# Two chunks of the first mixer's output through the staging tiles, and the spreading of queries and keys in code order on VectorE

## The chip, the cores and the metric

The kernel runs on one core of a Trainium2 chip. The metric is the device time of one execution in microseconds (us), from runs on the chip; a separate profiled execution gives the trace that is read here. TensorE does the matrix products, VectorE and ScalarE the elementwise work, GpSimd (POOL) and SyncE (SP) mainly issue transfers (DMAs). Each engine works through its own list of instructions in order and waits where an input, or the place for a result, is not ready.

## The reference

One step of a two-layer encoder, for 1024 new frames of one stream and 16 frames of each of 8 running streams (1152 tokens of width 1024). Cut to what matters here:

```python
# layer 0
h = rmsnorm(x, norm_mix[0])
q, k, v, a, g = split(h @ w_in_ab)              # 8 heads of 64; u = a * sigmoid(g)
z = (q @ k.T) / 8
w = exp(log_sigmoid(z) + sum of log_sigmoid(-z) over the later keys)   # masked: stick-breaking
a_out = w @ v
c_out = silu(layernorm(depthwise_conv31(u)))
x = x + concat(a_out, c_out) @ w_out_ab
x = x + square(relu(rmsnorm(x) @ w_up)) @ w_down
# layer 1: the same with chunk-band attention as the mixer; then a final rmsnorm
```

All products are in float32; most are made as three products of a high and a low part (`SPLIT`), which a `split` writes: the high part by ScalarE, the low part by VectorE.

## The kernel before

The first mixer (`mixer0`) goes over four pairs of heads, `p` = 0 to 3. A run of the loop over `p` attends pair `p` and, as filling work for TensorE, projects the queries, keys and values of pair `p + 1`. VectorE also has the taps of the depthwise convolution (L735), up to the end of pair 2; the convolution's layer norm runs in pair 3.

A pair is attended in 8 jobs (2 heads, 4 blocks of 256 queries). For each 128 queries TensorE makes the scores `z` (L924 to L927), ScalarE takes two sigmoids (L928, L929), VectorE makes a running product over the keys (the scan of `kp`, L907) and multiplies (`sg`, L909). Then TensorE transposes the weights (`tpa`, L388), ScalarE copies them out (L390), TensorE multiplies by the values (`ava`, L398), and ScalarE and VectorE add the two halves (`ata` L406, `cpa` L410). The result goes to the DRAM tile `cat_d` (L363), for pair 3 straight into the tiles `cat`. The transposes and products of a pair's last block (`carry`) are named at the head of the next run.

`expand` spreads the queries and keys of a pair before it is attended. For each of the two heads it makes the keys' high part on ScalarE (L348) and their low part on VectorE (L351), each copied to the other 64 partitions by a POOL DMA (L349, L352), and the queries' high part (L350, ScalarE) and low part (L353, VectorE). It reads the projected tiles `sq` and `sk`.

In pair 3's run the filling work is the output projection over the first three chunks of the mixer's output (`part_out`, products `psoa` with weights `wo0a`). Its operand comes back from `cat_d`: `ready_chunks` loads a chunk of 128x1152 into one tile of the tag `sk` (of which there is one, the same that held the projected keys) and splits it in three parts of 384 columns into `cat`. The `cat` tiles take the places of the normed input `h`, which the projections read. Chunks 0 and 1 come first, then the first products of the output projection, then chunk 2 (`late`, behind the last block of pair 2), and the rest.

Weights go through `staging`: a tile of the tag `st` (three of them, 128x512) that SP loads, and then a split into a pair `hl` (four of them).

What sets the order: `merge` and `level` write out one order from lists of steps with planned costs. The framework then makes each engine's list from this order by a planning model: the earlier-named instruction has priority, but one whose inputs are planned to be there sooner goes ahead of it. `tc.keep_in_program_order(ins)` puts an instruction behind the one named last before it on its engine.

Of the kernel before, what the change touches and what calls it, by code (L numbers as in the profile page):

```python
# [11 lines left out]
ALU = mybir.AluOpType  # L12
# [7 lines left out]
TP = 1024  # L20
TAPS = (26, 36, 38, 24)
G = 384
NG = 3
# [17 lines left out]
def f(ap):  # L41
    return ap.bitcast(F32)
# [82 lines left out]
def tile_trunk(ctx, tc, ins, outs):  # L125
    nc = tc.nc
    ACT = nc.scalar.activation
    tt = nc.vector.tensor_tensor
    stt = nc.vector.scalar_tensor_tensor
# [4 lines left out]
    def pool(name):  # L134
        return tc.tile_pool(name=name, bufs=1, reuse_waits="tile")
# [40 lines left out]
    cat_d = [dram.tile([KC, P, T], F32, name=f"cat_d{l}") for l in range(2)]  # L176
# [6 lines left out]
    def split(hi, lo, src):  # L183

        ACT(hi, src, AF.Copy)  # L185
        return tt(lo, src, f(hi), ALU.subtract)  # L186
# [3 lines left out]
    def staging(src, name, n=512):  # L190
        st = sp.tile([P, 512], F32, tag="st", name=f"st_{name}")
        dma(st[:, :n], src)
        return st
# [54 lines left out]
    chunks = {}  # L248
# [90 lines left out]
        return steps  # L339


    def expand(qs, kd, kl, q, k):


        for i in range(2):
            own = slice(64 * i, 64 * i + 64)
            oth = slice(64 - 64 * i, 128 - 64 * i)
            ACT(kd[i][own], k[own, :TP], AF.Copy)  # L348
            nc.gpsimd.dma_start(kd[i][oth], kd[i][own])  # L349
            ACT(qs[i][own], q[own, :TP], AF.Copy, scale=0.125)  # L350
            tt(kl[i][own], k[own, :TP], f(kd[i][own]), ALU.subtract)  # L351
            nc.gpsimd.dma_start(kl[i][oth], kl[i][own])  # L352
            stt(qs[i][oth], q[own, :TP], 0.125, f(qs[i][own]), ALU.mult, ALU.subtract)  # L353

    class Cat:

# [298 lines left out]
    def mixer0():  # L655
        with ExitStack() as st:
# [8 lines left out]
            pp = Bufs(st.enter_context(pool("pair0")))  # L665
# [77 lines left out]
            def ag(c):  # L743
                return (chunk_steps(at[16 + c], got, ahead, h, ks, lambda ps, g: gate(c, ps, g), f"g{c}")
                        + chunk_steps(at[12 + c], got, ahead, h, ks, lambda ps, g: value(c, ps, g), f"a{c}"))
# [124 lines left out]
            def proj(p):  # L870
                steps = []
                for n, tag in enumerate(("sq", "sk", "sv")):
                    def evac(ps, g, n=n, tag=tag):
                        if g == 0:
                            S[tag, p] = pp.tile([P, T], F32, tag, f"{tag}0{p}")
                        if g < 2:
                            tt(S[tag, p][:, g * G:g * G + G], ps[:, :G], rstd[g], ALU.mult)
                        else:
                            ACT(S[tag, p][:, g * G:], ps[:, :G], AF.Copy)
                        if g == 2 and n:  # L880
                            put(outs["sb_k" if n == 1 else "sb_v"][p], S[tag, p])
                    steps += chunk_steps(at[4 * n + p], got, ahead, h, ks, evac, f"p{p}{n}")
                return steps

            def expand_qk(p):
                q, k = S["sq", p], S["sk", p]
                expand(qs, kd, kl, q, k)
                S["qn"] = pp.tile([P, P], F32, "qn", f"qn0{p}")
                S["kn"] = pp.tile([P, P], F32, "kn", f"kn0{p}")
                ACT(S["qn"], q[:, TP:], AF.Copy, scale=0.125)  # L890
                ACT(S["kn"], k[:, TP:], AF.Copy)
# [69 lines left out]
            qs, kd, kl = ([ep.tile([P, TP], F32R, f"{n}{i}", f"{n}{i}") for i in range(2)] for n in "qkl")  # L961
# [3 lines left out]
            carry, cat_t = [], None  # L965
            for p in range(4):
                S["p"] = p
                expand_qk(p)
                if p < 3:
                    fill = proj(p + 1)  # L970
                    if p < 2:
                        fill[10:10] = ag(p + 2)
                    n = TAPS[p + 1]
                    mix, now, taps = [], taps[:n], taps[n:]
                else:
                    cat_t = new_hs("cat0")
                    (first, fill), now = part_out(0, range(3), pp, cat_t), []
                    for s in taps:
                        s.pe = 900.0
                    mix = taps + conv_norm(lambda: (conv_pool.close(), Bufs(st.enter_context(pool("ln")), t1=3, yl=5))[1],  # L980
                                           cat_t)
                cat = Cat(0, p, wk, cat_t)
                jobs = attend(p, cat)
                body, left = pipeline(jobs[1:], jobs[0][2])
                steps = carry + [jobs[0][0]] + [Step(327.0, lambda p=p, g=g: expand_v(p, g)) for g in range(NG)]
                if p == 3:
                    late, = ready_chunks(0, [2], pp, cat_t)
                    late.name, late.after, late.lag = "ready", carry[-1].name, 3000.0
                    fill[0].after, fill[0].lag = "ready", 5000.0
                    fill = ready_chunks(0, range(2), pp, cat_t) + first + [late] + fill  # L990
                steps += [jobs[0][1]] + body
                carry = left
                if p == 3:
                    steps += carry
                cs = sample_out(cat, wk, p)
                load = sample_caches(0, p, cp)
                sample = two_samples(*(sample_steps(0, p, bg, S, wk, load, soft, cs) for bg in range(2)))
                run(level(merge(steps, sample, fill, mix), now))
            return cat_t

    def conv_norm(new_pool, cat_t):

        steps = []

        pools = []

        def norm(g):
            box = {}

            def load():  # L1010
                if g == 0:
                    pools.append(new_pool())
                box["y"] = [pools[0].tile([P, G], F32, "yl", f"yl{g}{c}") for c in range(4)]
                for c in range(4):
                    put(box["y"][c], cat_d[0][4 + c, :, g * G:g * G + G])

            def centre():
                yl = box["y"]
                mu = bank(f"mu{g}")
                for c in range(4):  # L1020
                    mm(mu[:, :G], ones, yl[c], start=c == 0, stop=c == 3)
                for c in range(4):
                    stt(yl[c], mu[:, :G], -1.0 / 512, yl[c], ALU.mult, ALU.add)

            def squares():
                yl, box["acc"] = box["y"], None
                for c in range(4):
                    box["acc"] = add_square(box["acc"], yl[c], pools[0], f"l{g}{c}")

            def scale():  # L1030
                box["r"] = pools[0].tile([P, G], F32, "r", f"rl{g}")
                diag, box["rows"], _ = rstd_of(box["r"], pools[0], box["acc"], 1.0 / 512, LN_EPS, f"l{g}")
                diag(box["acc"])

            def out(c):
                y = box["y"][c]
                tt(y, y, box["r"], ALU.mult)
                s = pools[0].tile([P, G], F32, "t1", f"ls{g}{c}")
                gg, bb = cvec[:, 1, c:c + 1], cvec[:, 2, c:c + 1]
                ACT(s, y, AF.Sigmoid, bias=bb, scale=gg)  # L1040
                ACT(y, y, AF.Identity, bias=bb, scale=gg)
                tt(y, y, s, ALU.mult)
                split(cat_t[g][1][0][:, c, :], cat_t[g][1][1][:, c, :], y)

            name = f"ln{g}"
            return ([Step(50.0, load, 0.0, f"l{name}"),
                     Step(2600.0, centre, 1900.0, f"c{name}", f"l{name}", 4000), Step(500.0, squares, 1400.0),
                     Step(700.0, scale, 1200.0, f"s{name}", f"c{name}", 5000),
                     Step(800.0, lambda: box["rows"](), 0.0, None, f"s{name}", 2500)]
                    + [Step(300.0, lambda c=c: out(c), 1500.0) for c in range(4)])  # L1050

        for g in range(NG):
            steps += norm(g)
        return steps

    def ready_chunks(layer, chunks, pp, cat_t):

        steps = []
        for c in chunks:
            def go(c=c):  # L1060
                cr = pp.tile([P, T], F32, "sk", f"cr{layer}{c}")
                dma(cr, cat_d[layer][c])
                for g in range(NG):
                    hi, lo = (x[:, c % 4, :] for x in cat_t[g][c // 4])
                    split(hi, lo, cr[:, g * G:g * G + G])
            steps.append(Step(300.0, go))
        return steps
# [878 lines left out]
```

## Time and profile before

| | |
|---|---|
| time before, median of 3 runs | 2752.49 us (2751.73 to 2756.9) |
| the profiled execution | 2748.28 us |
| its span, first to last instruction | 2746.5 us |
| TensorE busy | 2666.7 us (97%) |
| VectorE busy | 2090.2 us (76%) |
| ScalarE busy | 1388.1 us (51%) |

The first mixer takes the first 550 us or so of the span. In the rows below PE is TensorE, PEld its weight loads, DVE VectorE, ACT ScalarE; L351 is line 351 of the kernel. Times are counted from the start of the span. "[4.14 <-DVE sg L909]" says that the engine was idle for 4.14 us before the instruction, and what ended that.

### The profile page before, as it was taken

Reading aid. Unit: us, or ns where it says so; the run is one execution under the profiler, and the core shown is the slowest. Engines: PE = TensorE matmul, PEld = TensorE weight load, DVE = VectorE, ACT = ScalarE, POOL = GpSimd, SP = SyncE. Lnnn points to the kernel's source line nnn. Section 1 sums busy time; section 2 is a strip of 40 time slices with the busy share of each in tenths; the row PEclk is TensorE's granted clock in tenths of the full one; section 3 lists DMA queues with packets and bytes.
Section 4 is the critical chain, followed back from the end, with each engine's and each line's share of the span. In section 5 each row is a group of like instructions: output and inputs, shape, how many; then the busy total and the mean of one; then the engine's idle time right before and its main releaser. Section 6 shows DMA issues by size and latency. Waiting matters only on the chain.

```text
span 2746.5 us, 50585 instructions
## 1 busy us (share of the span) xinstructions
PE 2666.7 (97%) x19362; PEld 2553.7 (93%) x19362; DVE 2090.2 (76%) x4117; ACT 1388.1 (51%) x2906; POOL 328.2 (12%) x599
## 2 busy tenths in 40 slices
PE   8999898999999999999999999998999999999998
PEld 8987776799999999999999999997999999999998
DVE  8999998888777755768577777778787777647577
ACT  5344457755444543435355555556555545434344
POOL 1000101041111100000011111110221111100001
PEclk9999999999999999999999999999999999999999
DMA  4434446454344377435444444446534334674344
GB/s 158 124 113 141 122 137 228 144 176 140 142 143 145 133 271 248 118 102 174 141 138 144 133 139 139 132 134 231 180 127 144 143 140 144 232 259 134 96 125 145
DMA packets 173203, 422.90 MB, mean 154 GB/s; under 512 B 25968, under 2 KB 53808, under 8 KB 170912
## 3 DMA queue, kind: packets, MB, share of 16 engines
q1 hardware_dynamic: 135696, 288.38, 33.4%
q0 software_dynamic: 37120, 131.27, 13.9%
q8 instruction: 152, 2.49, 0.4%
q14 instruction: 91, 0.75, 0.1%
q10 hardware_dynamic: 144, 0.02, 0.0%
HBM read 289.60 MB, written 117.34 MB: 148 GB/s over the span
## 4 chain that ended last, share of the span: by engine, by line
PE 71%; DVE 4%; ACT 2%; DMA 1%; issue 1%; DVEq 0%; SPq 0%; ACTq 0%; POOLq 0%
PE pd L1690 26%; PE um L1461 25%; PE psc L225 10%; PE avc L467 2%; PE tpc L455 2%; PE zc L1201 1%; PE zc L1202 1%; PE psoa L225 1%; PE so L602 1%; PE zs L568 1%; DVE xr L1367 0%; PE psob L225 0%; DMA cr<-cat_d 0%; ACT s L1168 0%; ACT whc L185 0%
## 5 line engine op out<-in xcount | busy, mean ns | idle before, releaser
L225 PE MATMUL psc<-h,hl_wc 128*128 128x384 f32 x1728 | 327.2, 340 | 0.0
L225 PEld LDWEIGHTS psc<-h,hl_wc 128*128 128x128 f32 x1728 | 296.9, 188 | 13.3 <-issue 10.9
L1461 PE MATMUL um<-sl,hl_m 128*128 128x288 f32 x1548 | 240.8, 296 | 0.0
L1461 PEld LDWEIGHTS um<-sl,hl_m 128*128 128x128 f32 x1548 | 218.2, 189 | 0.0
L1690 PE MATMUL pd<-tm,hl_wd 128*128 128x288 f32 x1584 | 214.7, 295 | 0.0
L1690 PEld LDWEIGHTS pd<-tm,hl_wd 128*128 128x128 f32 x1584 | 211.3, 189 | 0.0
L735 DVE SCALAR_TENSOR_TENSOR y<-u,dw,y 128x1024 f32<-128x1024 f32 (+1 forms) x232 | 178.1, 810 | 0.6
L225 PE MATMUL psp<-h,hl_wi 128*128 128x384 f32 x864 | 165.7, 344 | 0.0
L1468 ACT ACTIVATE hdm<-hdm 128x288 f32<-128x288 f32 x192 | 84.7, 442 | 156.5 <-DVE hdm L1467 154.8
L225 PEld LDWEIGHTS psp<-h,hl_wi 128*128 128x128 f32 x864 | 150.8, 191 | 6.8 <-issue 6.0
L186 DVE TENSOR_TENSOR tm<-xr,tm 128x576 fp32r<-128x576 f32 (+1 forms) x120 | 86.1, 718 | 92.4 <-ACT tm L185 92.3
L185 ACT ACTIVATE tm<-xr 128x576 fp32r<-128x576 f32 (+1 forms) x120 | 77.6, 647 | 94.7 <-PE pd L1690 76.2
L1168 ACT ACTIVATE s<-s,mxc 128x640 f32<-128x640 f32 (+4 forms) x128 | 88.8, 694 | 60.2 <-DVE mxc L1165 58.5
L1461 PE MATMUL um<-sl,hl 128*128 128x288 f32 x756 | 119.1, 296 | 0.0
L1690 PE MATMUL pd<-th,hl_wd 128*128 128x288 f32 x792 | 113.9, 297 | 4.0 <-DVE th L186 3.9
L1690 PEld LDWEIGHTS pd<-th,hl_wd 128*128 128x128 f32 x792 | 108.4, 190 | 4.9 <-DVE th L186 4.3
L1690 PE MATMUL pd<-xr,hl_wd 128*128 128x288 f32 x792 | 112.3, 296 | 0.0
L1690 PEld LDWEIGHTS pd<-xr,hl_wd 128*128 128x128 f32 x792 | 107.8, 190 | 0.0
L1461 PEld LDWEIGHTS um<-sl,hl 128*128 128x128 f32 x756 | 106.4, 188 | 0.8
L1690 PE MATMUL pd<-tm,hl 128*128 128x288 f32 x768 | 104.9, 295 | 0.0
L1690 PEld LDWEIGHTS pd<-tm,hl 128*128 128x128 f32 x768 | 103.1, 188 | 0.0
L185 ACT ACTIVATE whc<-tpc 128x512 fp32r<-128x512 f32 (+1 forms) x144 | 72.3, 522 | 46.6 <-PE tpc L455 44.8
(526 smaller groups left out, 6632.1 us busy)
## 6 DMA issues: line engine op xcount, KB each, us to landing
xr<-hb_d SPq DMA_DIRECT2D x208, 288.0 KB, 3.0
xr<-in_w_up_dram SPq DMA_DIRECT2D x64, 512.0 KB, 4.3
hb_d<-hdm POOLq DMA_DIRECT2D x96, 288.0 KB, 2.4
hb_d<-t POOLq DMA_DIRECT2D x96, 288.0 KB, 2.4
wm<-in_w_down_dram SPq DMA_DIRECT2D x64, 256.0 KB, 4.0
st_wd<-in_w_down_dram SPq DMA_DIRECT2D x64, 256.0 KB, 3.7
st_wc<-in_w_in_c_dram SPq DMA_DIRECT2D x44, 256.0 KB, 3.0
xm_d<-xo POOLq DMA_DIRECT2D x16, 576.0 KB, 3.5
```

The lines of the kernel that those rows point to most:

```text
L185: ACT(hi, src, AF.Copy)
L186: return tt(lo, src, f(hi), ALU.subtract)
L225: mm(ps()[:, :G], hl[:, a, at:at + P], act[g][k // 4][b][:, k % 4, :], start=n == 0, stop=n == len(todo) - 1)
L455: nc.tensor.transpose(tp[:, c0 + q * P:c0 + (q + 1) * P], blocks.get(j, tile_q), ident)
L467: mm(st["av"][:, o0:o0 + n], vs[:, j, i].rearrange("p a d -> p (a d)"), src[:, c0:c0 + n], start=st["done"] == 0, stop=st["done"] == nmm - 1)
L568: mm(box["z"][at // 512][own, at % 512:at % 512 + kw], qb[:, own], k[:, b * kw:b * kw + kw], start=True, stop=True)
L602: mm(box["o"][own, 0:P], wt[k4][:, c:c + 32], v[:, at:at + P], start=False, stop=k4 == nz - 1 and j == 3)
L735: stt(src if j == CW - 1 else dst, src, wj, dst, ALU.mult, ALU.add)
L1168: ACT(s[:, :n], s[:, :n], AF.Exp, bias=mx, scale=-1.0, accum_out=tot)
L1461: mm(banks[b, n][:, :TQ], w[:, a, c * P:c * P + P], combo(key, c)[:, h, n * TQ:n * TQ + TQ], start=k < 3 and c == 0 and i == 0, stop=c == ...
L1468: ACT(y, y, AF.Relu)
L1690: mm(ps, w[:, a, m * P:m * P + P], b[:, h, (n - ns[0]) * TQ:(n - ns[0]) * TQ + TQ], start=first and s == 0, stop=j == NJ - 1 and s == 2, s ...
```

## The change

It does two things. `expand` gets an argument `pin`; in the first mixer, for pairs 1 to 3, it is `keep_in_program_order`, and it is laid on the two VectorE instructions of each head (keys' and queries' low parts). And chunks 0 and 1 of the first mixer's output come back in pieces of 384 columns by a new function, `ready_pieces`: each piece is loaded into a staging tile and split from there; a step is one piece and not one chunk. Chunk 2 stays as it was.

```diff
-    def expand(qs, kd, kl, q, k):
+    def expand(qs, kd, kl, q, k, pin=lambda ins: ins):
...
-            tt(kl[i][own], k[own, :TP], f(kd[i][own]), ALU.subtract)
+            pin(tt(kl[i][own], k[own, :TP], f(kd[i][own]), ALU.subtract))
             nc.gpsimd.dma_start(kl[i][oth], kl[i][own])
-            stt(qs[i][oth], q[own, :TP], 0.125, f(qs[i][own]), ALU.mult, ALU.subtract)
+            pin(stt(qs[i][oth], q[own, :TP], 0.125, f(qs[i][own]), ALU.mult, ALU.subtract))
...
-                expand(qs, kd, kl, q, k)
+                expand(qs, kd, kl, q, k, *([tc.keep_in_program_order] if p else []))
...
-                    fill = ready_chunks(0, range(2), pp, cat_t) + first + [late] + fill
+                    fill = ready_pieces(0, range(2), cat_t) + first + [late] + fill
...
+    def ready_pieces(layer, chunks, cat_t):
+
+        def go(c, g):
+            st = staging(cat_d[layer][c, :, g * G:g * G + G], f"cr{layer}{c}{g}", G)
+            split(*(x[:, c % 4, :] for x in cat_t[g][c // 4]), st[:, :G])
+
+        return [Step(100.0, lambda c=c, g=g: go(c, g)) for c in chunks for g in range(NG)]
```

## Rows read from the trace of the kernel before

**Rows 1.** Busy us (x instructions) of PE, PEld, DVE, ACT, POOL by stretch; clock; DMA.
```profile
214.00:335.00 121.00, 109.22 (x800) 93.60 (x800) 116.44 (x157) 55.51 (x129) 11.64 (x21) 0.97 0.45 130
335.00:420.00 85.00, 81.00 (x640) 67.56 (x641) 83.66 (x110) 47.07 (x113) 7.53 (x14) 0.98 0.41 126
...
446.00:580.00 134.00, 127.16 (x868) 108.98 (x865) 116.35 (x209) 100.95 (x215) 20.44 (x28) 0.99 0.56 187
```
**Rows 2.** Waits of TensorE, 90 to 450 us: total us, times, longest.
```profile
PE tpa L388 <- DVE sg L909: 21.5, 9, 6.2
```
**Rows 3.** VectorE in order of time at pair 0 to 1: start, us, instruction.
```profile
211.51 1.21 DVE L351 TENSOR_TENSOR l<-sk,k 64x1024 fp32r<-64x1024 f32 x1
...
214.95 1.22 DVE L351 TENSOR_TENSOR l<-sk,k 64x1024 fp32r<-64x1024 f32 x1
216.20 1.22 DVE L909 TENSOR_TENSOR sg<-sg,kp 128x1023 f32<-128x1023 f32 x1
```
**Rows 4.** ScalarE in order of time at pair 2 to 3.
```profile
421.07 0.62 ACT L929 ACTIVATE kp<-z 128x512 f32<-128x512 f32 x1
```
**Rows 5.** VectorE in order of time at pair 2 to 3.
```profile
422.08 1.22 DVE L351 TENSOR_TENSOR l<-sk,k 64x1024 fp32r<-64x1024 f32 x1
423.34 1.22 DVE L353 SCALAR_TENSOR_TENSOR q<-sq,q 64x1024 fp32r<-64x1024 f32 x1
424.59 2.29 DVE L907 TENSOR_TENSOR_SCAN kp<-kp,ones 128x1024 f32<-128x1024 f32 x1
...
426.91 1.23 DVE L909 TENSOR_TENSOR sg<-sg,kp 128x1023 f32<-128x1023 f32 x1
...
428.43 0.42 DVE L410 TENSOR_TENSOR cpa<-ava,ata 64x256 f32<-64x256 f32 x1
...
431.20 1.50 DVE L186 TENSOR_TENSOR cat<-cr,cat 128x384 fp32r<-128x384 f32 x3 [1.29 <-ACT cat L185]
```
**Rows 6.** TensorE in order of time at pair 2 to 3.
```profile
428.19 0.87 PE L388 MATMUL tpa<-ident,sg 128*128 128x128 f32 x6 [4.14 <-DVE sg L909]
431.22 0.69 PE L225 MATMUL psoa<-cat,hl_wo0a 128*128 128x384 f32 x1 [2.15 <-ACT cat L185]
...
439.48 2.44 PE L225 MATMUL psoa<-cat,hl_wo0a 128*128 128x384 f32 x12
...
444.30 0.33 PE L924 MATMUL z<-k,q 128*128 128x128 f32 x1
```
**Rows 7.** SP's DMA issues in order of time, 360 to 450 us.
```profile
365.02 0.89 SPq L192 DMA_DIRECT2D st_wo0a<-in_w_out_ab_dram  x2
...
423.33 0.34 SPq L1062 DMA_DIRECT2D cr<-cat_d  x1
...
432.72 0.33 SPq L1062 DMA_DIRECT2D cr<-cat_d  x1
```
**Rows 8.** DMA issues, 420 to 442 us: KB each, median us to landing.
```profile
cr<-cat_d SPq DMA_DIRECT2D x2, 576.0 KB, 6.7
...
st_wo0a<-in_w_out_ab_dram SPq DMA_DIRECT2D x2, 192.0 KB, 5.5
l<-l POOLq DMA_DIRECT2D x1, 256.0 KB, 7.0
```
**Rows 9.** Busy us by stretch, as rows 1, around pair 2 to 3.
```profile
422.00:440.00 18.00, 11.71 (x61) 7.01 (x61) 9.75 (x15) 6.74 (x15) 6.32 (x11) 0.81 1.08 348
...
428.00:444.30 16.30, 13.95 (x80) 8.73 (x80) 7.69 (x17) 7.71 (x16) 3.77 (x7) 0.79 0.83 284
```
**Rows 10.** Spreading that ran early on VectorE: first and last of five.
```profile
153.24 1.22 DVE L353 SCALAR_TENSOR_TENSOR q<-sq,q 64x1024 fp32r<-64x1024 f32 x1
...
396.21 1.21 DVE L351 TENSOR_TENSOR l<-sk,k 64x1024 fp32r<-64x1024 f32 x1
```
**Rows 11.** DMA issues, 360 to 400 us, as rows 8.
```profile
st_wo0a<-in_w_out_ab_dram SPq DMA_DIRECT2D x4, 192.0 KB, 2.5
...
l<-l POOLq DMA_DIRECT2D x1, 256.0 KB, 2.9
```

## The prediction, made before the result was known

> **What bounds the kernel now.** I read the busy times by stretch first, because the whole page only says that TensorE is busy 97% of the span. The stretch in question is the first mixer. While pairs 1 and 2 are attended (214 to 420 us), VectorE is busy in 116.44 of 121 and 83.66 of 85 us: it is idle for 4.56 + 1.34 = 5.9 us of 206, and TensorE for 11.78 + 4.00 = 15.8 us. After the mixer's hand-over to pair 3 (446 to 580 us) it is TensorE that is full, 127.16 of 134 us [rows 1]. So up to 420 us VectorE sets the pace, and time saved at the hand-over should be carried through what follows. The list of waits says what TensorE waits for between 90 and 450 us: 21.5 us in 9 waits for the last VectorE step of a block's stick-breaking weights (`sg`, L909) [rows 2].
>
> Then I read VectorE and TensorE in order of time around the two hand-overs that the change touches most.
>
> At pair 0 to 1, VectorE spreads the next pair's keys (L351, 1.21 us) ahead of the last block's scan, and a second time (1.22 us) between the scan and the product that TensorE's transposes need; the product starts at 216.20 [rows 3]. That is the 6.2 us wait, the longest of rows 2.
>
> At pair 2 to 3 it is plainer. The scan's input was finished by ScalarE at 421.07 + 0.62 = 421.69 [rows 4], but VectorE runs L351 at 422.08 and L353 at 423.34 first; the scan starts at 424.59, the product ends at 426.91 + 1.23 = 428.14 [rows 5], and TensorE's transposes resume at 428.19 after 4.14 us of idleness [rows 6]. Next TensorE waits 2.15 us for chunk 0 of `cat`, and its last 12 products with `cat` start only at 439.48; the first product of pair 3's scores is at 444.30, behind them in TensorE's order [rows 6]. Chunk 0 is late because its load was issued at 423.33, when L351 had read the keys' tile `sk` that it lands in, and chunk 1 is late because it shares that tile: issued at 432.72 [rows 7]. Both take 6.7 us to land, where transfers of a third the size take 5.5 us [rows 8]: from 422 to 440 us the 16 DMA engines are busy 1.08 of the time, so everything lands late [rows 9].
>
> **The pin.** It removes and adds no instruction; it moves twelve (four for each of pairs 1 to 3). By the order in which the code names the work, the last VectorE instruction named before `expand_qk(p)` is the addition at L410 of the previous pair's last block but one (428.43 at pair 2 to 3 [rows 5]), so the four now run in a row behind it: 4 x 1.22 = 4.9 us. Some had run far earlier: the first is at 153.24, the last of that kind at 396.21, five in all [rows 10].
>
> Count the work ahead of the product that ends at 428.14. Before, all twelve stand ahead of it. After, pair 3's four stand behind it, the eight of pairs 1 and 2 still ahead. So VectorE has 4 x 1.22 = 4.9 us less to do before that point. Of this, 424.59 - 422.08 = 2.5 us is the direct part (the scan follows the taps at once). The other 2.4 us (pair 3's first two, the later of them at 396.21 [rows 10]) counts only if TensorE and ScalarE follow, for ScalarE's 421.69 leaves no more than 0.4 us otherwise. They can: TensorE's waits of rows 2 are waits for VectorE. From below the value is 2.5 us, if the rest is lost in the order of things; from above, the 4.9 us plus what late work can fill of VectorE's idle time, taken as 2.4 of the 5.9 us of rows 1, so 7.3. I take 4.9, since VectorE is idle for only 1.34 of 85 us in the stretch just before [rows 1]. The gain at pair 0 to 1 (216.20 - 213.82 = 2.4 us, if a scan of 2.29 us [rows 5] starts at 211.51) is not an extra: the four moved instructions run right after it, in the same full stretch.
>
> What the pin makes late: the spread keys' second half is copied by a DMA behind L351, and pair 3's scores need it. L351 would run near 424, and with 7.0 us of landing [rows 8] and POOL's issue it is there by 432: ahead of 444.30, so it costs nothing unless the scores are wanted 12 us sooner than now. In POOL's queue the copy stands ahead of the loads of the convolution's rows, which are wanted after it. At a quieter hand-over the copy takes 2.9 us [rows 11], and there the next pair's projection fills TensorE meanwhile.
>
> **The staging.** Two loads of 576 KB into `sk` become six of 192 KB into the `st` tiles; the same six splits of 128x384 remain (1.50 us of VectorE for a chunk's three [rows 5], as many on ScalarE). SP issues four more loads, at some 0.35 us each [rows 7], 1.4 us on an engine that is mostly idle; it lies beside SP's waiting. What falls away is the wait for `sk`: the first three pieces can land as soon as staging tiles are free, and the output weights (`st_wo0a`), which come behind them in the code, took theirs at 365.02 already [rows 7], with 2.5 us to land in that quiet time [rows 11]. So chunk 0 is there when the projection lets go of the `h` tiles it is written to, and the 2.15 us wait goes.
>
> But the kernel has three staging tiles. The second three pieces and then the output weights must wait until the first pieces are split. The chain is: three lo splits 1.5, landing 2.5 to 5.5, splits 1.5, weights landing 2.5 to 5.5, their split some 1.1 (two such instructions); 9.1 us in quiet and 15.1 in crowded time [rows 5, 8, 11]. If the lo splits start near 419, when VectorE finishes its taps in the shifted kernel, the 18 products can start at 428 to 434, ahead of 439.48. If they come behind the four pinned instructions (near 429), at 438 to 444.
>
> For the hand-over after the product I read one stretch: from 428 to 444.30 TensorE is busy 13.95 of 16.30 us at a granted clock of 0.79, so it loses 2.35 us idle and up to 0.21 x 16.3 = 3.4 us because part ran at 1.2 and not 2.4 GHz, after it had been idle since 424 [rows 9]. At best the change gains both, 5.8 us; at worst the chain costs 6 us or more. I take 1.1 us, half the wait for chunk 0: in the middle of the first case, since the chain still makes TensorE wait for something.
>
> **A rule weighed.** In rows 8 and 11 a piece of 192 KB lands in 2.5 us in quiet time and 5.5 us in crowded time. The Trainium skill, "DMA: Bandwidth & Descriptors", section "Anatomy of one DMA", gives a fixed cost of about 2.0 us for each transfer plus its bytes over 436 GB/s, which speaks against cutting two transfers into six. By it a piece (197 kB) would take 2.45 us, which the quiet row bears out; if all six were waited for one by one, it would be four more fixed costs, 8 us more and a slower kernel. The sum here does without it: three pieces are in flight at once, and in crowded time the row decides.
>
> **Sum.** 4.9 + 1.1 = 6.0 us. The profiled execution took 2748.28 us (span 2746.5 and 1.8 around it); less 6.0 that is 2742.3. The median of the runs is 2752.49, 4.2 above the profiled one; in its terms the forecast is 2746.5.
>
> **Rivals.** A change under 0.2% (5.5 us) can hardly be told from none here.
> - *The staging chain replaces the wait (slower).* If VectorE takes the lo splits behind the pinned four and the loads land at crowded times, the output products start at 444 instead of 439.48. They end at 448, the scores follow 2.4 us later, near 450.4 and not 444.30, and an idle TensorE drops to 1.2 GHz again as in rows 9, for some 2.5 us: 6.1 + 2.5 = 8.6 us slower, 2761. It decides once the weights are split after 439.5. For it speak the three tiles; against it, that TensorE's order may put pair 3's scores first. Chance 0.15.
> - *The chain eats the gain.* The weights come near 437 to 440; 4 of the 6 us go. 2750.5. Chance 0.2.
> - *Only moved.* VectorE fills the freed places with taps that wanted to be run anyway, and the last scan comes no more than 2.5 us sooner, with the wait for chunk 1 in place of that for chunk 0: 2750. Rows 1 speak for it (work is conserved), rows 4 and 5 against. Chance 0.15.
>
> **Numbers.** The forecast has 0.5, with its own range from 4 to 11 us less, 2741.5 to 2748.5; about a fifth of it lies within 0.2%. Faster: 0.42. Same: what is left of the forecast, 0.08, and both middle rivals, 0.35, so 0.43. Slower: 0.15. The range takes in the forecast's lower half and two thirds of the slower case: 2741 to 2757.
>
> **What would show it.** Right: at pairs 0 to 1 and 2 to 3 the scan follows the last tap with no L351 or L353 ahead; the four stand in a row behind L410; the list of waits for `sg` falls from 21.5 to some 16 us; three pieces land before 400 us; the first scores of pair 3 come near 438. Wrong: `st_wo0a` loads issued after 430 with TensorE waiting for their splits, or lo splits of `cat` ahead of the last scan, which would give its gain back.

## The result, and the profile after

The changed kernel takes 2762.23 us in the median of 7 runs, the kernel before 2752.49 us beside it; the ratio is 1.0028, with a 95% interval of 1.0018 to 1.0038. So it is slower by 0.28%, 7.7 us by the ratio. (The ratio is taken over all the runs and is not the quotient of the two medians, which lie 9.7 us apart; all sizes below go by ratios.) The forecast was 2746.5 us, with a range up to 2757: wrong in sign and outside the range. The profiled execution took 2757.41 us, 9.1 more than the one before, and its span grew by the same 9.1, to 2755.6.

Where this arises is read from events that both traces have. Attention of pair 2 begins (its first `vt` transposes) 3.3 us earlier than before, the last `sg` of pair 2 ends 1.4 us earlier, and the first scores of pair 3 come 9.5 us later (453.78 against 444.30 [rows 6]). What follows keeps a delay of some 9 to 11 us to the end. The whole loss lies between the last `sg` and the first scores: 10.9 us in one hand-over.

The list of TensorE's waits between 90 and 460 us names it: total us, times, longest.

```profile
PE tpa L388 <- DVE sg L909: 16.7, 7, 5.1
PE psoa L225 <- ACT hl_wo0a L185: 12.5, 1, 12.5
```

The waits for `sg` fell from 21.5 to 16.7 us, as forecast for the pin. But there is a new wait of 12.5 us, for the high part of the output weights. Before, at this place, TensorE waited 2.15 us for `cat` [rows 6].

TensorE of the changed kernel in order of time (start, us, instruction, and in brackets how long it was idle and what ended that):

```profile
426.81 1.54 PE L388 MATMUL tpa<-ident,sg 128*128 128x128 f32 x6 [4.41 <-DVE sg L909]
...
440.85 2.29 PE L225 MATMUL psoa<-cat,hl_wo0a 128*128 128x384 f32 x6 [12.50 <-ACT hl_wo0a L185]
...
449.90 1.51 PE L225 MATMUL psoa<-cat,hl_wo0a 128*128 128x384 f32 x6
...
453.78 0.33 PE L924 MATMUL z<-k,q 128*128 128x128 f32 x1
```

The transposes resume 1.4 us earlier than in [rows 6]; then nothing until 440.85. The wait grew by 12.50 - 2.15 = 10.35 us, and the gap ahead of the transposes by 4.41 - 4.14 = 0.27: together 10.6 of the 10.9.

What the weights waited for stands in SP's issues (start, time over which they were issued, count):

```profile
332.79 0.34 SPq L192 DMA_DIRECT2D st_cr<-cat_d  x1
...
363.61 0.88 SPq L192 DMA_DIRECT2D st_cr<-cat_d  x2
...
422.38 1.91 SPq L192 DMA_DIRECT2D st_cr<-cat_d  x3
...
433.33 12.17 SPq L192 DMA_DIRECT2D st_wo0a<-in_w_out_ab_dram  x7
```

Chunk 0's three pieces took the three staging tiles at 332.79 and 363.61, when these came free, because the code names them ahead of the output weights. Their parts go where the projection's `h` lies until late in pair 2: ScalarE made the high parts at 414.45 and VectorE, behind its taps, the low parts at 421.81. So the three staging tiles were held for 58 to 89 us. At 422.38 the second chunk's pieces took them over, and the output weights, which before were loaded at 365.02 [rows 7], were issued at 433.33.

VectorE in order of time shows why the second round lasted until then:

```profile
420.35 1.54 DVE L735 SCALAR_TENSOR_TENSOR u<-u,dw,y 128x1024 f32<-128x1024 f32 x2
421.81 1.49 DVE L186 TENSOR_TENSOR cat<-st_cr,cat 128x384 fp32r<-128x384 f32 x3
423.21 2.28 DVE L907 TENSOR_TENSOR_SCAN kp<-kp,ones 128x1024 f32<-128x1024 f32 x1
425.53 1.23 DVE L909 TENSOR_TENSOR sg<-sg,kp 128x1023 f32<-128x1023 f32 x1
427.04 0.42 DVE L410 TENSOR_TENSOR cpa<-ava,ata 64x256 f32<-64x256 f32 x1
427.49 1.22 DVE L351 TENSOR_TENSOR l<-sk,k 64x1024 fp32r<-64x1024 f32 x1
428.74 1.22 DVE L353 SCALAR_TENSOR_TENSOR q<-sq,q 64x1024 fp32r<-64x1024 f32 x1
429.97 1.22 DVE L351 TENSOR_TENSOR l<-sk,k 64x1024 fp32r<-64x1024 f32 x1
431.23 1.22 DVE L353 SCALAR_TENSOR_TENSOR q<-sq,q 64x1024 fp32r<-64x1024 f32 x1
432.48 1.50 DVE L186 TENSOR_TENSOR cat<-st_cr,cat 128x384 fp32r<-128x384 f32 x3
440.83 1.54 DVE L186 TENSOR_TENSOR hl_wo0a<-st_wo0a,hl_wo0a 128x384 fp32r<-128x384 f32 x3 [6.85 <-ACT hl_wo0a L185]
```

Two things are to be seen. Chunk 0's low parts (421.81) run ahead of the last scan, which starts at 423.21 and not when the taps end. And the second chunk's low parts wait behind the four pinned instructions, until 432.48. ScalarE had made the first high part at 426.00, as soon as its piece landed, and the third at 430.05:

```profile
426.00 0.52 ACT L185 ACTIVATE cat<-st_cr 128x384 fp32r<-128x384 f32 x1 [3.53 <-DMA st_cr<-cat_d]
...
430.05 0.52 ACT L185 ACTIVATE cat<-st_cr 128x384 fp32r<-128x384 f32 x1 [0.74 <-DMA st_cr<-cat_d]
...
440.27 1.50 ACT L185 ACTIVATE hl_wo0a<-st_wo0a 128x384 fp32r<-128x384 f32 x3 [9.22 <-DMA st_wo0a<-in_w_out_ab_dram]
```

The weights, issued from 433.33 on, were split from 440.27: 6.9 us for the first of them. So the chain from chunk 0's low parts to the first product is 440.85 - 421.81 = 19.0 us.

Busy us (x instructions) of PE, PEld, DVE, ACT, POOL by stretch of the changed kernel, then the granted clock and the DMA share:

```profile
422.00:440.00 18.00, 1.95 (x9) 1.31 (x8) 11.78 (x15) 3.03 (x6) 6.79 (x12) 0.59 0.91 267
...
425.60:445.80 20.20, 6.49 (x28) 4.77 (x29) 10.27 (x14) 5.54 (x11) 4.32 (x8) 0.50 0.72 218
...
446.00:580.00 134.00, 127.06 (x877) 104.79 (x876) 113.25 (x207) 99.37 (x214) 16.80 (x25) 0.99 0.55 184
```

From 422 to 440 us TensorE is busy 1.95 us where it was 11.71 [rows 9]. The clock is 0.50, the lower level of 1.2 GHz, for 20.2 us, and TensorE is busy for 6.49 of them. From 446 to 580 us TensorE is as full as before, 127.06 against 127.16 of 134 [rows 1], so the delay is not made up there.

### The profile page after: what moved, and what is told of

Read it like the earlier page. It is cut to its first block, busy times and chain, and to the rows that moved or that the text cites. A ratio compares the mean times of both kernels' runs of the same rounds, so it can differ in the third digit from the quotient of the medians.

```text
span 2755.6 us, 50598 instructions
## 1 busy us (share of the span) xinstructions
PE 2669.1 (97%) x19362; PEld 2556.0 (93%) x19362; DVE 2090.3 (76%) x4117; ACT 1388.5 (50%) x2906; POOL 328.8 (12%) x599
## 4 chain that ended last, share of the span: by engine, by line
PE 78%; DVE 12%; ACT 4%; issue 3%; DMA 3%; POOL 0%; SPq 0%; DVEq 0%; ACTq 0%; POOLq 0%
PE pd L1698 26%; PE um L1469 25%; PE psc L225 10%; DVE y L735 3%; PE psp L225 3%; PE avc L467 2%; DVE kp L907 2%; PE tpc L455 2%; PE psoa L225 1%; PE f L225 1%; PE zc L1209 1%; PE psob L225 1%; PE zc L1210 1%; DVE sg L909 1%; PE so L602 1%
## 5 line engine op out<-in xcount | busy, mean ns | idle before, releaser
L225 PEld LDWEIGHTS psc<-h,hl_wc 128*128 128x128 f32 x1728 | 296.8, 188 | 13.3 <-issue 10.9
```

Source lines behind the costliest of these rows:

```text
L225: mm(ps()[:, :G], hl[:, a, at:at + P], act[g][k // 4][b][:, k % 4, :], start=n == 0, stop=n == len(todo) - 1)
```

## The experiments

Each kernel was timed in turns with the kernel before; the ratio is to that, with its 95% interval. The diffs are against the changed kernel, but for "The rows on SP in the kernel before". Between two experiments I compare ratios. Times within one trace are single executions, and those differ by some 2 us where nothing was edited: the first scan starts between 106.92 and 109.06 us in the twelve traces, and with the rows on SP in the kernel before, an edit that lies behind it, the last `sg` of pair 2 starts at 428.89, where [rows 5] have 426.91. Five of the ten measured times (the pieces alone, weights first without the pin, the rows on SP, chunk 0 alone, and the last one) lie 0.2 to 1.7 us outside the range expected; each still falls on the side of the theory that its waits bear out.

### The pin alone

```diff
-                    fill = ready_pieces(0, range(2), cat_t) + first + [late] + fill
+                    fill = ready_chunks(0, range(2), pp, cat_t) + first + [late] + fill
```

> The pin alone; both chunks come back through sk as before. Theory S (the serial chain through three staging tiles makes the change slower): the 12.5 us wait of TensorE for the split output weights is gone, since those weights find free staging tiles near 365 us again. Theory P (the pin itself makes it slower): the wait stays, and the time stays near 2762. Under S there is still a price: the load of chunk 0 waits until the second L351 has read sk, which the pin puts near 431 and not 423, so the first product with cat comes some 5 us later than before the change: 2752 to 2758. Lower than 2750 would say that the pin alone is a gain.

Measured: 2755.11 us beside 2752.93, ratio 1.0007 [0.9996, 1.0017]. The waits of TensorE, 90 to 460 us:

```profile
PE psoa L225 <- ACT cat L185: 8.8, 1, 8.8
...
PE tpa L388 <- DVE sg L909: 15.8, 7, 5.2
```

The wait for `sg` is down by 5.7 us, but the wait for chunk 0 is 8.8 where it was 2.15 [rows 6]. Its load was issued at 429.14, and at 423.33 before [rows 7]: it lands in the keys' tile `sk`, and the pinned L351 reads that tile from 427.83 to 429.05. So the pin moves the last reading of `sk` back by some 6 us and with it chunk 0. This cost of the pin by itself the prediction did not have. It also says what the staging is good for: it takes chunk 0 off `sk`.

### The pieces alone

```diff
-                expand(qs, kd, kl, q, k, *([tc.keep_in_program_order] if p else []))
+                expand(qs, kd, kl, q, k)
```

> The pieces alone, no pin. Under S the output weights still come last through the three tiles, so TensorE waits for them at pair 2 to 3; but chunk 1's low parts no longer stand behind four spreading instructions on VectorE (2 to 5 us of the chain), so the wait is 6 to 10 us and not 12.5, and the time 2754 to 2760. Under P: no wait for the weights and the time of before, 2752, or less.

Measured: 2760.21 us beside 2752.93, ratio 1.0026 [1.0017, 1.0035]. The waits, and SP's issues:

```profile
PE tpa L388 <- DVE sg L909: 22.6, 8, 6.2
PE psoa L225 <- ACT hl_wo0a L185: 9.4, 1, 9.4
```

```profile
433.15 1.64 SPq L192 DMA_DIRECT2D st_cr<-cat_d  x3
...
437.93 9.39 SPq L192 DMA_DIRECT2D st_wo0a<-in_w_out_ab_dram  x7
```

The staging makes the kernel slower by itself, as much as the whole change. Without the pin, chunk 0's low parts run behind the spreading and the last `sg`, at 432.56, so the second chunk's pieces are issued at 433.15 and the weights at 437.93; the wait is shorter only because TensorE arrives at it later. The chain sets the start of the products in both cases, so the pin is worth nothing that shows: 1.0026 without, 1.0028 with.

### The output weights claim the staging tiles first

`first` begins with the step that stages the output weights; it is named ahead of the pieces, and nothing else changes.

```diff
-                    fill = ready_pieces(0, range(2), cat_t) + first + [late] + fill
+                    fill = first[:1] + ready_pieces(0, range(2), cat_t) + first[1:] + [late] + fill
```

> As the change, but the step that loads the first two output weights is named ahead of the pieces, so they take staging tiles first. Under S the 12.5 us wait for their split goes and 8 to 12 us come back: 2750 to 2754, or less if the pin's gain (2.4 us at each hand-over) is kept. Under P it stays near 2762.

Measured: 2752.26 us beside 2752.93, ratio 0.9996 [0.9985, 1.0007]. Against the change this is 0.0032 of the time, 8.8 us, from the order of two steps: the whole loss. TensorE in order of time:

```profile
419.62 0.84 PE L225 MATMUL psoa<-cat,hl_wo0a 128*128 128x384 f32 x3
...
424.23 0.98 PE L388 MATMUL tpa<-ident,sg 128*128 128x128 f32 x6 [3.56 <-DVE sg L909]
...
437.90 1.08 PE L1021 MATMUL mu<-yl,ones 128*128 128x384 f32 x2 [2.38 <-DMA yl<-cat_d]
...
440.54 0.48 PE L924 MATMUL z<-k,q 128*128 128x128 f32 x1
```

The first products with `cat` run at 419.62, even ahead of the last `sg`, and the first scores come at 440.54, 3.8 us ahead of [rows 6]. Yet the time is that of the kernel before. In this execution (2754.80 us, 2.5 above the median) the windows say where the 3.8 us went:

```profile
434.00:438.00 4.00, 1.62 (x9) 0.68 (x7) 0.00 (x0) 0.00 (x0) 0.00 (x0) 1.00 1.07 320
...
440.40:444.00 3.60, 2.76 (x19) 1.62 (x16) 1.70 (x5) 3.04 (x8) 0.55 (x1) 0.50 0.57 164
444.00:448.00 4.00, 3.40 (x15) 3.10 (x14) 3.11 (x8) 3.54 (x11) 0.00 (x0) 0.50 0.66 191
448.00:452.00 4.00, 3.31 (x18) 2.45 (x19) 4.00 (x6) 3.51 (x9) 0.00 (x0) 0.50 0.88 341
```

TensorE waits 2.38 us for the convolution's rows `yl`, and its clock then is 0.50 in the next stretches, while it is busy for 9.47 of the 11.6 us from 440.40 to 452. In the kernel before the clock was 1.00 there:

```profile
438.00:456.00 18.00, 15.49 (x107) 11.07 (x106) 14.15 (x25) 12.76 (x32) 0.55 (x1) 1.00 0.67 210
```

That the clock costs as much in other executions of this kernel is not shown.

### Weights first, without the pin

```diff
-                expand(qs, kd, kl, q, k, *([tc.keep_in_program_order] if p else []))
+                expand(qs, kd, kl, q, k)
...
-                    fill = ready_pieces(0, range(2), cat_t) + first + [late] + fill
+                    fill = first[:1] + ready_pieces(0, range(2), cat_t) + first[1:] + [late] + fill
```

> Pieces with the weights named first, and no pin: against e3_weights_first it gives what the pin is worth when the staging chain is out of the way. Under S 2750 to 2755, and the pin's worth up to 5 us either way; under P faster than e3_weights_first by 8 us or more.

Measured: 2755.34 us beside 2752.93, ratio 1.0008 [0.9999, 1.0017]. Against weights first with the pin (0.9996) the pin is worth 0.0012, 3.3 us; the intervals overlap, so it is a likely size only. Against the pieces alone (1.0026) the order of the two steps is worth 0.0018, 5.0 us, without the pin too.

### Weights first, and the convolution's rows on SP's queue

The loads of `yl` stand in POOL's queue (`put`); here SP issues them (`dma`).

```diff
-                    fill = ready_pieces(0, range(2), cat_t) + first + [late] + fill
+                    fill = first[:1] + ready_pieces(0, range(2), cat_t) + first[1:] + [late] + fill
...
-                    put(box["y"][c], cat_d[0][4 + c, :, g * G:g * G + G])
+                    dma(box["y"][c], cat_d[0][4 + c, :, g * G:g * G + G])
```

> As e3_weights_first, and the loads of the convolution's rows (yl) are issued by SP and not by POOL, where they stood behind the pinned keys' copies and landed at 437.9. Theory Q (with the staging chain out of the way, these loads are the next thing TensorE waits for, because the pin delays POOL's queue): the 2.4 us wait of the mu products goes, pair 3's scores come before 440, and the time falls to 2747 to 2750. Rival C (the crowded DMA engines set it, whoever issues): the rows land as late, and the time stays within 2 us of e3_weights_first, 2750 to 2754.

Measured: 2745.32 us beside 2754.0, ratio 0.9969 [0.996, 0.9979]. This is faster than both kernels. In weights first, POOL issued the last two loads only at 429.70, behind the copy of the pinned keys, which waited for VectorE's L351:

```profile
429.18 0.53 POOL L352 DMA_DIRECT2D l<-l  x1 [1.06 <-DVE l L351]
429.70 1.09 POOL L1015 DMA_DIRECT2D yl<-cat_d  x2
```

With the loads on SP, four are issued between 423.23 and 428.44:

```profile
423.23 5.21 SPq L1015 DMA_DIRECT2D yl<-cat_d  x4
```

TensorE in order of time, and its clock by stretch:

```profile
432.36 2.20 PE L1021 MATMUL mu<-yl,ones 128*128 128x384 f32 x6 [0.39 <-DMA yl<-cat_d]
...
438.67 0.33 PE L924 MATMUL z<-k,q 128*128 128x128 f32 x1
```

```profile
431.00:436.00 5.00, 4.61 (x22) 3.12 (x18) 3.46 (x7) 1.36 (x3) 0.39 (x1) 1.00 1.11 254
436.00:440.00 4.00, 4.00 (x39) 2.36 (x41) 2.55 (x6) 1.49 (x4) 0.54 (x1) 1.00 1.08 339
440.00:444.00 4.00, 1.64 (x15) 1.10 (x8) 1.71 (x4) 2.71 (x8) 0.00 (x0) 0.93 0.74 236
444.00:448.00 4.00, 3.95 (x21) 2.94 (x21) 2.83 (x7) 3.82 (x14) 0.00 (x0) 0.50 0.99 307
448.00:452.00 4.00, 4.00 (x19) 3.81 (x18) 3.96 (x3) 3.97 (x7) 0.00 (x0) 0.71 0.93 327
```

The last sums `mu` of the convolution's norm end at 432.36 + 2.20 = 434.56, which is 4.4 us sooner than with weights first alone (437.90 + 1.08 = 438.98); the first of them start no sooner. The scores come at 438.67, which is 5.6 us ahead of [rows 6], and the stretch at the lower clock is shorter (0.93, 0.50, 0.71 over 440 to 452, and not 0.50 throughout). Against weights first alone the ratio falls by 0.0027, 7.4 us, and the wait that went was 2.4 us. The clock may account for the rest, but that is read from one execution of each kernel (this one took 2749.32 us, 4 above the median).

### Chunk 0 alone in pieces

Chunk 1 goes through `sk` again, so only one round of pieces stands ahead of the weights.

```diff
-                    fill = ready_pieces(0, range(2), cat_t) + first + [late] + fill
+                    fill = ready_pieces(0, range(1), cat_t) + ready_chunks(0, [1], pp, cat_t) + first + [late] + fill
```

> As the change, but only chunk 0 comes in pieces; chunk 1 comes through sk as before, behind it. The order of pieces ahead of weights stays. Theory S1 (it is the second set of pieces that makes the weights late: two turns through three tiles): the weights are loaded near 422, right behind the first pieces' low parts, and the 12.5 us wait is gone, but chunk 1's load waits for the pinned reading of sk near 430 and its products for 437 or so: 2753 to 2757. Rival S2 (any pieces ahead of the weights are enough): the wait of 10 us or more stays, 2760 or more.

Measured: 2751.96 us beside 2754.0, ratio 0.9992 [0.9982, 1.0001]. SP's issues, then TensorE:

```profile
422.93 1.80 SPq L192 DMA_DIRECT2D st_wo0a<-in_w_out_ab_dram  x3
...
432.33 0.33 SPq L1070 DMA_DIRECT2D cr<-cat_d  x1
```

```profile
428.55 0.99 PE L225 MATMUL psoa<-cat,hl_wo0a 128*128 128x384 f32 x2
...
441.26 1.74 PE L225 MATMUL psoa<-cat,hl_wo0a 128*128 128x384 f32 x4 [2.90 <-ACT cat L185]
```

With one round the weights are issued 10.4 us sooner (422.93 for 433.33), the first products start at 428.55, and 0.0036 of the time, 9.9 us, comes back against the change. So it is the second round ahead of the weights that cost the time. What limits now is chunk 1, late through `sk` as in the kernel before: 2.90 us of waiting.

### Weights first, the pin for pair 3 alone

```diff
-                expand(qs, kd, kl, q, k, *([tc.keep_in_program_order] if p else []))
+                expand(qs, kd, kl, q, k, *([tc.keep_in_program_order] if p == 3 else []))
...
-                    fill = ready_pieces(0, range(2), cat_t) + first + [late] + fill
+                    fill = first[:1] + ready_pieces(0, range(2), cat_t) + first[1:] + [late] + fill
```

> As e3_weights_first, with the pin at pair 3 alone. If the pin's gain comes from the last hand-over, where four spreading instructions leave VectorE's full stretch, the time equals e3_weights_first within 1.5 us (2751 to 2754). If it comes from the waits at pairs 0 to 1 and 1 to 2, the time is that of e6_weights_first_nopin, 2754 to 2757.

Measured: 2755.06 us beside 2754.0, ratio 1.0002 [0.9991, 1.0013]. It stands between weights first with the whole pin (0.9996) and without (1.0008), and its interval takes in both. So in the time it stays open how the pin's gain divides among the hand-overs. The trace says more. VectorE's last `sg` of pair 2, and TensorE's busy time and clock later on:

```profile
424.57 1.23 DVE L909 TENSOR_TENSOR sg<-sg,kp 128x1023 f32<-128x1023 f32 x1
```

```profile
440.40:457.40 17.00, 14.49 (x69) 11.28 (x68) 13.22 (x24) 14.10 (x33) 0.55 (x1) 0.50 0.65 218
```

From the first scan of the trace (108.64) to this `sg` it is 315.9 us. It is 315.9 with the whole pin and 322.5 without, each with the weights first. So up to the last `sg` the pin of pair 3 does alone what the whole pin does, as the forecast counted it. Behind it comes a wait of 2.1 us for `yl` and a clock of 0.50, as with weights first.

### The rows on SP in the kernel before

```diff
-                    put(box["y"][c], cat_d[0][4 + c, :, g * G:g * G + G])
+                    dma(box["y"][c], cat_d[0][4 + c, :, g * G:g * G + G])
```

> The kernel before, with only the loads of the convolution's rows issued by SP. If the gain of e7_yl_on_sp (0.3%) were that move's alone, this is 2744 to 2748. If the move pays only once the staging chain and the reading of sk are out of the way (in the kernel before, the wait for chunk 1 of cat stands behind the mu products, not they behind it), it stays within 3 us of before: 2750 to 2756.

Measured: 2753.61 us beside 2753.98, ratio 1.0 [0.9991, 1.0009]. The loads are no limit there: TensorE waits for `cat`, 5.4 us in two waits, the longest 3.3.

### The rows on SP in the changed kernel

```diff
-                    put(box["y"][c], cat_d[0][4 + c, :, g * G:g * G + G])
+                    dma(box["y"][c], cat_d[0][4 + c, :, g * G:g * G + G])
```

> The change, with only that move of the loads to SP. The staging chain stands first in TensorE's order, so the wait for the split output weights stays 10 us or more and the time 2757 to 2764. Under the rival that POOL's queue was what made the change slow, it falls to 2750 or less.

Measured: 2759.86 us beside 2753.98, ratio 1.0022 [1.0012, 1.0031]. TensorE still waits for the weights:

```profile
439.97 2.29 PE L225 MATMUL psoa<-cat,hl_wo0a 128*128 128x384 f32 x6 [11.53 <-ACT hl_wo0a L185]
```

So the move of the loads pays neither here (1.0022 beside 1.0028, and the intervals overlap) nor in the kernel before; it pays where the weights come first and chunk 0 is off `sk`. From here to weights first with the rows on SP (0.9969) it is 0.0053, 14.6 us: by one reordering, the dearest step of the study.

### Weights first and rows on SP, without the pin

```diff
-                expand(qs, kd, kl, q, k, *([tc.keep_in_program_order] if p else []))
+                expand(qs, kd, kl, q, k)
...
-                    fill = ready_pieces(0, range(2), cat_t) + first + [late] + fill
+                    fill = first[:1] + ready_pieces(0, range(2), cat_t) + first[1:] + [late] + fill
...
-                    put(box["y"][c], cat_d[0][4 + c, :, g * G:g * G + G])
+                    dma(box["y"][c], cat_d[0][4 + c, :, g * G:g * G + G])
```

> As e7_yl_on_sp, without the pin: what the pin is worth in the best version. By the forecast's 4.9 us less work ahead of pair 2's last scan it is 3 to 5 us slower than e7_yl_on_sp: 2748 to 2751. If the pin does nothing of its own, it equals e7_yl_on_sp within 1.5 us.

Measured: 2751.65 us beside 2753.98, ratio 0.9989 [0.998, 0.9999]. The pin is worth 0.9989 - 0.9969 = 0.0020 here, 5.5 us, beside a forecast of 4.9. The wait for `sg`, which is 16.2 us with the pin, is back:

```profile
PE tpa L388 <- DVE sg L909: 20.2, 9, 6.2
```

From the first scan to the last `sg` of pair 2 it is 322.0 us here and 315.7 with the pin. Over all the traces it is 319.8 to 322.5 us in the five without a pin, 314.7 to 315.9 in the four with a pin and the weights not behind the pieces, and 317.0 to 318.4 in the three (the change among them) that have a pin and the pieces ahead of the weights.

Against weights first without the pin (1.0008) the move of the rows to SP is worth 0.0019, 5.2 us, with no pin in either. There POOL issued the rows only from 434.22, behind the write-backs to `cat_d` (L363), the first of which had waited for VectorE. So the copy of the pinned keys is one thing that holds the rows back in POOL's queue, and not the only one.

## Why the prediction was wrong

**The step that failed** is the end of the part on the staging: "I take 1.1 us, half the wait for chunk 0: in the middle of the first case." With the pin in both, the staging cost 1.0028 - 1.0007 = 0.0021, 5.8 us, where the sum had a gain of 1.1. The start of that case was told rightly. The low parts of chunk 0 started at 421.81, near the 419 that the first case assumed; but the products started at 440.85, and not at 428 to 434, because the chain lasted 19.0 us and not 9.1 to 15.1.

Against its upper bound of 15.1 us (1.5 + 5.5 + 1.5 + 5.5 + 1.1) the chain was 3.9 too long. From the first low part to the last piece's landing it took 430.05 - 421.81 = 8.2 us, for 1.5 + 5.5 = 7.0. Then comes a term that the sum did not have: the second pieces' low parts stood behind the four pinned instructions, until 432.48, 2.4 us. The prediction had this order as a second case (products at 438 to 444) for the first pieces alone; it hit the second ones. The weights were issued 0.85 us later, for 1.5, since the first tile is free before the last split. They took 433.33 to 440.27, 6.9 us, for 5.5, though the DMA share of 0.91 between 422 and 440 us was lower than the 1.08 of [rows 9]. The first product followed 0.6 us on, for 1.1. So the landing times of [rows 8] were no upper bound, and the place of a split in VectorE's list was left out: 1.2 + 2.4 - 0.65 + 1.4 - 0.5 = 3.9.

**What was seen and priced too low** is the larger thing. Before, the weights had been loaded at 365.02 [rows 7] and were waiting for the products. In the change they are last in a line for three tiles, and the tiles are held from 332.79 and 363.61 by pieces whose low parts were made only at 421.81. The prediction named the three tiles as what spoke for a rival, and credited the early pieces as a gain. That the weights, and not the pieces, were the ones to go first was shown by swapping the two (8.8 us).

**The slower rival** was the mechanism that came: its point was weights split after 439.5 (they were split at 440.27), its time 2761 (measured 2762.23), its price 8.6 us (measured 7.7). It was given 0.15. That the price fits is partly luck: the products started at 440.85, 3.2 us before the rival's 444, and the scores came at 453.78, 3.4 us after its 450.4, because all the work behind the first product was still to be done and not only the last twelve products.

**The pin** was right in its mechanism. The scan follows directly in the hand-over 0 to 1 (taps at 208.68, scan at 210.14, `sg` at 212.92, and L351 at 215.71), the four stand in a row at 427.49 to 432.45, and the waits for `sg` fell to 16.7 as said. Its size was near 4.9: 5.5 and 3.3 us where the weights come first, the second with overlapping intervals. In the change's time nothing of it shows, since TensorE waits for the weights whatever `sg` does; and in its trace the last `sg` came only 1.4 us sooner (2.8 without the low parts of chunk 0 ahead of the scan). VectorE, which the prediction took to be full, was there idle for 85.00 - 79.12 = 5.9 us from 335 to 420, where it had been 1.34 [rows 1], and for 1.1 with the weights first. One wait for ScalarE's `ata` (L406), 3.8 us up to 397.28, is most of it. The two other kernels with the pin and the pieces ahead of the weights have the same wait (3.8 and 2.3 us), the other kernels do not; why it comes with that order stays open. One cost was missed that the change hides: by itself the pin keeps `sk` busy and delays chunk 0's load (the pin alone, 8.8 us of waiting). So each half of the change spoils something that the other half, or the order, would have to mend.

**"Lo splits of `cat` ahead of the last scan"** was named as a sign of failure, and came: chunk 0's, 1.4 us. It is the smallest part. In the version that is faster than both kernels the same three run at 420.92, ahead of the scan at 422.33.

**The rule on the fixed cost of a transfer** (the Trainium skill, "DMA: Bandwidth & Descriptors", section "Anatomy of one DMA") would, if all six were waited for one by one, have given a kernel 8 us slower (an estimate), which is near what was measured, but not by that way. Six transfers in place of two, with the weights first, take the time of the kernel before (0.9996), and less with the rows on SP. The section is on transfers that GpSimd issues, and these are issued by SP. And where an estimate by the rule gives 2.45 us for 192 KB, these landed in 5.9 and 6.4 us in the median here; the measurement decides, for this crowded stretch.

**Left open:** how the pin's gain in time divides among the hand-overs, how much of the times behind the last `sg` is due to the clock, and what more staging tiles would do, which was not tried.

## What to carry to other kernels

When a transfer is moved to a small pool of shared buffers, ask not only when it lands, but how long it holds its place: here a buffer was claimed in the order of the code and held until its last reader had run. What can be used up at once, or is needed first, should be named first. Here the pieces that came early and waited 58 to 89 us kept out the weights that the next products needed, and the swap of two steps was worth 8.8 us.

A chain of load, split and load again is priced with the landing times of the crowded stretch in which it runs, and with the place of every split in its engine's list. And two edits that each look good alone are to be tried apart, and with the next obstacle removed: the pin was worth nothing that shows in the change, and some 5.5 us once the weights and the rows were on time.

## What the runs showed of the hardware

Here the late start cost TensorE a second time, by its clock. In the changed kernel the clock was 0.50 for 20.2 us, from 425.60 to 445.80, after an idle time that began at 422.4. In the 6.49 us in which TensorE was busy, six products with `cat` took 2.29 us (at 440.85); six took 1.51 us at 449.90, at the full clock. At the full clock the 6.49 us would be at least half as long, so the price is at most some 3.2 us (an estimate), and the 2.5 us in the slower rival were about right.

With the weights first TensorE was busy 1.62 of 4.00 us from 434 to 438; from 440.40 to 452.00 the clock was 0.50, and TensorE was busy 9.47 of the 11.6 us. By the same estimate this costs up to 4.7 us, which is enough to take back the 3.8 us won in the start of the scores. With the pin for pair 3 alone the clock was 0.50 from 440.40 to 457.40. With the rows on SP TensorE was busy 8.61 of the 9.00 us from 431 to 440 and 1.64 of 4.00 from 440 to 444; the clock was 0.50 from 444 to 448, and 0.71 from 448 to 452. These are single executions, and what sets the clock is not shown by them.
